# The float steps of an inverse square root on another engine: an encoder layer with 40 small calls of it

## The chip, the cores and the metric

The kernel runs on one core of a Trainium2 chip. A core has a matmul engine (TensorE, PE in the profile; its weight loads are PEld), a vector engine (VectorE, DVE), a scalar engine (ScalarE, ACT), a general engine (GpSimd, POOL) and a queue that issues most of the transfers (SyncE, SP). Each engine works through its own list of instructions in order; where one needs what another makes, it waits on a semaphore. The metric is the time of one execution on the device, in microseconds.

## The reference

One encoder layer is applied to two sequences, of 1024 and of 2048 tokens of width 1024, each with 16 learned meta tokens in front:

```python
xn = _rmsnorm(h, g_pre)
proj = xn @ w_in + b_in
ya = neighbourhood_attention(...) * silu(na_z) @ w_a      # 8 heads of 64
yb = mlstm(...) normalised per head * silu(ml_z) @ w_b    # 4 heads of 128, both directions
y = (ga * ya + gb * yb) @ w_out
return h + _rmsnorm(y, g_post)
```

An inverse square root is wanted at three places: for each token in the first norm of x, for each token and mLSTM head in the head norm (mean and variance over 128 channels), and for each token in the last norm. In each the argument is one number per token, so it has 128 partitions and 1 to 4 columns.

## The kernel before

All matmuls are made in pairs of a high and a low part (`mm3`, lines 141 to 146: three products for one), so most tiles are split by one ScalarE copy and one VectorE subtraction. Weights are loaded raw, split once (`wpump`, from line 221; the first three low parts are made by POOL, the others by VectorE, line 238) and kept in DRAM for later use.

Two generators are interleaved by estimated cost. The dense one (`dense`, `group`, `final`) makes the projections of x in halves of 512 tokens and, at the end of each sequence, the output projections in blocks of 512 tokens. The sparse one (`sparse`) makes the mLSTM of the prompt, its attention, then both of the sample. The instruction list of TensorE is exactly this order. Those of VectorE, ScalarE, POOL and SyncE are planned by the framework's scheduler from the data flow, with an estimate of each instruction's time, when the program is built; a changed instruction can therefore change the order of others on these engines.

The inverse square root is `rsqrt8` (line 125): an integer shift and an integer subtraction from a magic constant give a first guess (lines 130, 131), and three Newton passes of three VectorE instructions each improve it (lines 133 to 135). It is called 40 times from three places:

- `build_half`, line 295, 7 calls. 512 tokens of x are loaded in tiles `xr`, squared and summed by ScalarE (L292), the sums go through `rsqrt8`, VectorE scales x by the result (L298), TensorE transposes x (L309), ScalarE and VectorE split the transpose into `xh` (L311) and `xl` (L312). The first two calls stand at the start of the kernel, before any projection can be made.
- `ml_norm`, line 1193, 24 calls, one for each mLSTM head and 512 tokens. VectorE gates the head's output `hb` (L1184), takes its mean and variance (L1188, L1190), adds the epsilon (L1192); `rsqrt8` follows; VectorE normalises (four L1196) and gates again (L1197); eight steps of the generator later TensorE transposes the tile (L1202), ScalarE scales it (L1203), and it is stored.
- `final_out`, line 1369, 9 calls: five for 512 tokens at once, and in the last block of the sample one for each 128 tokens. ScalarE sums the squares of a block's output from PSUM (L1327), VectorE multiplies it by the gain (L1328), the sums are added (L1367, L1368), `rsqrt8` follows, VectorE scales and adds the input `xres` (L1373, twice for 128 tokens), and the result is stored (L1374). The four loads' buffers are reused, so a later `xres` is loaded when an earlier L1373 is done.

POOL does little else: it clears small tiles (L289, L361, L838, L840, L982 and others), copies 16 columns of meta keys (L362, L363), splits the three first weights, and issues the transfers of the attention's masks (L558, L636).

Of the kernel before, what the change touches and what calls it, by code (L numbers as in the profile page):

```python
# [13 lines left out]
ALU = mybir.AluOpType  # L14
# [96 lines left out]
class K:  # L111
# [13 lines left out]
    def rsqrt8(self, pool, v, shape):  # L125

        nc = self.nc
        y = pool.tile(shape, F32, name="nwy", bufs=2)
        t = pool.tile(shape, F32, name="nwt", bufs=2)
        nc.vector.tensor_scalar(y.bitcast(I32), v.bitcast(I32), 1, None, op0=ALU.logical_shift_right)  # L130
        nc.vector.tensor_scalar(y.bitcast(I32), y.bitcast(I32), -1.0, MAGIC, op0=ALU.mult, op1=ALU.add)
        for n in range(3):
            nc.vector.scalar_tensor_tensor(t, y, 0.25 ** n, y, op0=ALU.mult, op1=ALU.mult)
            nc.vector.tensor_tensor(t, t, v, op=ALU.mult)
            nc.vector.scalar_tensor_tensor(y, t, 3.0, y, op0=ALU.subtract, op1=ALU.mult)
        return y

    def psum(self, tag, shape):
# [1349 lines left out]
```

## Time and profile before

| | |
|---|---|
| median of 3 runs | 2904.53 us (2902.79 to 2905.13) |
| the profiled execution | 2912.43 us |
| its span on the core | 2910.7 us |
| TensorE busy | 2820.4 us, 97% |
| VectorE busy | 1749.4 us, 60% |
| ScalarE busy | 1293.7 us, 44% |
| POOL busy | 23.4 us, 1% |
| mean granted clock of TensorE | 0.989 |

The profile is one execution recorded by the hardware. Start times and durations are in us from the start of the span; `L133` is line 133 of the kernel; `nwt<-nwy` gives the tile written and the tiles read, then partitions x elements. `nwy` and `nwt` are the two tiles of `rsqrt8`. A note like `[12.93 <-DVE hb L1197]` behind a row says that the engine sat idle for 12.93 us before it and that VectorE's L1197 ended the wait. `x2` behind a row merges two like instructions. Durations of POOL are rough.

### The profile page before, as it was taken

The numbers are of one execution on the slowest core, as the hardware profiler recorded it, in microseconds if no ns is written. First come the engines' busy times: TensorE is split into PE (matmuls) and PEld (weight loads), VectorE is DVE, ScalarE is ACT, GpSimd is POOL, SyncE is SP. The second block draws the span as 40 slices with busy tenths as digits, with TensorE's granted clock in tenths as the row PEclk, the third lists the DMA queues.
The fourth block names the chain that finished last, engine by engine and source line by source line (L and its number), as shares of the span: only waits on it lengthen the run. The fifth ranks groups of instructions, "written<-read, shape, count | busy, mean of one in ns | idle before, by whom it ended". The sixth has DMA issues, their size and how long they took to land.

```text
span 2910.7 us, 49314 instructions
## 1 busy us (share of the span) xinstructions
PE 2820.4 (97%) x17488; PEld 2513.6 (86%) x17488; DVE 1749.4 (60%) x4813; ACT 1293.7 (44%) x3114; POOL 23.4 (1%) x107
## 2 busy tenths in 40 slices
PE   6999999999999999999998999999999999999998
PEld 6998898899789988888886988898888888889887
DVE  5232576666556755467669778463555557777843
ACT  4112555444343444355655545453444445545421
POOL 1000000000000000000000000000000000000000
PEclk9999999999999999999999999999999999999999
DMA  9655576754775553578779798546659659888975
GB/s 349 221 178 180 198 230 235 269 185 161 246 233 171 186 170 123 173 249 273 233 249 316 265 341 293 176 140 196 200 180 293 207 166 262 259 289 253 304 255 193
DMA packets 436888, 661.88 MB, mean 227 GB/s; under 512 B 51136, under 2 KB 257296, under 8 KB 436640
## 3 DMA queue, kind: packets, MB, share of 16 engines
q1 hardware_dynamic: 435520, 656.03, 68.9%
q0 software_dynamic: 1120, 2.69, 0.4%
q8 instruction: 138, 2.26, 0.3%
q14 instruction: 110, 0.90, 0.1%
HBM read 447.97 MB, written 210.61 MB: 226 GB/s over the span
## 4 chain that ended last, share of the span: by engine, by line
PE 83%; DMA 9%; DVE 5%; ACT 1%; issue 1%; SPq 0%; DVEq 0%; ACTq 0%
PE pj L144 14%; PE pj L145 14%; PE pj L146 14%; PE pj L409 6%; PE pj L410 6%; PE pj L411 6%; PE sm L700 3%; PE pj L1302 3%; PE pj L1300 3%; PE pj L1301 3%; PE tr L688 3%; PE sc L663 1%; PE sc L664 1%; DMA tg<-gt 1%; PE sm L146 1%
## 5 line engine op out<-in xcount | busy, mean ns | idle before, releaser
L144 PE MATMUL pj<-xh,whi 128*128 128x512 f32 (+1 forms) x1824 | 717.1, 393 | 0.2 <-DVE xl L312 0.2
L145 PE MATMUL pj<-xl,whi 128*128 128x512 f32 (+1 forms) x1824 | 700.3, 384 | 0.4 <-DVE xl L312 0.4
L146 PE MATMUL pj<-xh,wlo 128*128 128x512 f32 (+1 forms) x1824 | 698.5, 383 | 0.0
L409 PE MATMUL pj<-whi,xh 128*128 128x256 f32 (+3 forms) x1576 | 451.8, 287 | 0.0
L410 PE MATMUL pj<-wlo,xh 128*128 128x256 f32 (+3 forms) x1576 | 445.7, 283 | 0.0
L411 PE MATMUL pj<-whi,xl 128*128 128x256 f32 (+3 forms) x1576 | 445.4, 283 | 0.0
L146 PEld LDWEIGHTS pj<-xh,wlo 128*128 128x128 f32 x1824 | 343.9, 189 | 72.1
L144 PEld LDWEIGHTS pj<-xh,whi 128*128 128x128 f32 x1824 | 344.3, 189 | 57.7 <-DVE xl L312 0.8
L145 PEld LDWEIGHTS pj<-xl,whi 128*128 128x128 f32 x1824 | 344.7, 189 | 55.6 <-DVE xl L312 0.7
L409 PEld LDWEIGHTS pj<-whi,xh 128*128 128x128 f32 (+1 forms) x1576 | 295.5, 188 | 1.5 <-issue 0.2
L410 PEld LDWEIGHTS pj<-wlo,xh 128*128 128x128 f32 (+1 forms) x1576 | 295.2, 187 | 1.1
L411 PEld LDWEIGHTS pj<-whi,xl 128*128 128x128 f32 (+1 forms) x1576 | 295.1, 187 | 0.9
L1300 PE MATMUL pj<-whi,mh 128*128 128x256 f32 x768 | 221.7, 289 | 0.0
L671 ACT ACTIVATE prb<-sc,mx 128x384 f32<-128x384 f32 (+2 forms) x192 | 120.1, 625 | 228.1 <-DVE mx L667 221.3
L1302 PE MATMUL pj<-whi,mlo 128*128 128x256 f32 x768 | 218.8, 285 | 1.9 <-DVE mlo L1283 1.9
L1301 PE MATMUL pj<-wlo,mh 128*128 128x256 f32 x768 | 218.4, 284 | 0.0
L691 DVE TENSOR_TENSOR pts<-tr,pts 96x512 fp32r<-96x512 f32 (+2 forms) x192 | 131.9, 687 | 119.2 <-ACT pts L690 117.5
L418 DVE TENSOR_TENSOR stT<-pj,bb 128x256 f32<-128x256 f32 (+3 forms) x197 | 83.3, 423 | 153.7 <-PE pj L411 150.4
L690 ACT ACTIVATE pts<-tr 96x512 fp32r<-96x512 f32 (+2 forms) x192 | 114.0, 594 | 115.9 <-PE tr L688 115.6
L667 DVE CUSTOM_DVE_ANT_1 sc<-sc,gt 128x384 f32<-128x384 f32 (+2 forms) x192 | 118.7, 618 | 76.1 <-PE sc L664 68.3
L144 PE MATMUL pj<-yh,whi 128*128 128x512 f32 x384 | 157.0, 409 | 7.4 <-DVE tg L1279 7.3
L706 DVE TENSOR_TENSOR yg<-sm,yg 64x128 f32<-64x128 f32 x384 | 108.3, 282 | 77.7 <-ACT yg L704 70.1
(233 smaller groups left out, 5123.7 us busy)
## 6 DMA issues: line engine op xcount, KB each, us to landing
whi<-wh SPq DMA_DIRECT2D x176, 512.0 KB
wlo<-wl SPq DMA_DIRECT2D x176, 512.0 KB
wh<-whi SPq DMA_DIRECT2D x64, 512.0 KB
wl<-wlo SPq DMA_DIRECT2D x64, 512.0 KB
wraw<-w_in SPq DMA_DIRECT2D x48, 512.0 KB
gt<-st SPq DMA_DIRECT2D x96, 256.0 KB
tg<-gt SPq DMA_DIRECT2D x96, 256.0 KB
xh<-xh SPq DMA_DIRECT2D x6, 2048.0 KB
```

The costliest lines, as they stand in the source:

```text
L144: mm(out, ah, bh, start=start, stop=False)
L145: mm(out, ah, bl, start=False, stop=False)
L146: mm(out, al, bh, start=False, stop=stop)
L409: nc.tensor.matmul(o, xh, wh, start=k == 0, stop=False)
L410: nc.tensor.matmul(o, xh, wl, start=False, stop=False)
L411: nc.tensor.matmul(o, xl, wh, start=False, stop=k == KT - 1)
L667: nc.vector.tensor_tensor_reduce(out=so, in0=so, in1=gt[:, g0:g0 + ns, c0:c0 + 32], op0=ALU.add, op1=ALU.min, scale=-1.0, scalar=3.0e38, a ...
L671: nc.scalar.activation(pr_[:, :N].rearrange("p (b a c) -> p b a c", b=4, c=8), sc[:, :N].rearrange("p (a b c) -> p b a c", b=4, c=8), AF.E ...
L691: nc.vector.tensor_tensor(pts[:ks, :, 1, :], pt[:ks], pts[:ks, :, 0, :].bitcast(F32), op=ALU.subtract)
L1300: nc.tensor.matmul(o, mh[:, k, xs], wh, start=k == 0, stop=False)
L1301: nc.tensor.matmul(o, mh[:, k, xs], wl, start=False, stop=False)
L1302: nc.tensor.matmul(o, ml[:, k, xs], wh, start=False, stop=k == KT - 1)
```

## The change

Only the Newton passes change engine and form. The two integer steps stay on VectorE. Each pass was three VectorE instructions, of which two fold a constant in; it becomes four POOL instructions, since the constant and the subtraction of 3 are made by an instruction of their own. The values are the same up to rounding. A call so issues 2 instructions on VectorE and 12 on POOL, where it issued 11 on VectorE.

```diff
@@ -130,9 +130,10 @@
         nc.vector.tensor_scalar(y.bitcast(I32), v.bitcast(I32), 1, None, op0=ALU.logical_shift_right)
         nc.vector.tensor_scalar(y.bitcast(I32), y.bitcast(I32), -1.0, MAGIC, op0=ALU.mult, op1=ALU.add)
         for n in range(3):
-            nc.vector.scalar_tensor_tensor(t, y, 0.25 ** n, y, op0=ALU.mult, op1=ALU.mult)
-            nc.vector.tensor_tensor(t, t, v, op=ALU.mult)
-            nc.vector.scalar_tensor_tensor(y, t, 3.0, y, op0=ALU.subtract, op1=ALU.mult)
+            nc.gpsimd.tensor_tensor(t, y, y, op=ALU.mult)
+            nc.gpsimd.tensor_tensor(t, t, v, op=ALU.mult)
+            nc.gpsimd.tensor_scalar(t, t, 0.25 ** n, -3.0, op0=ALU.mult, op1=ALU.add)
+            nc.gpsimd.tensor_tensor(y, t, y, op=ALU.mult)
         return y
```

## The prediction

> **What bounds the kernel now.** I read the page first, then TensorE's waits, then every instruction that touches the two small tiles of the inverse square root, and last the timeline at the places where TensorE waits behind one.
>
> ```profile
> span 2910.7 us, 49314 instructions
> PE 2820.4 (97%) x17488; PEld 2513.6 (86%) x17488; DVE 1749.4 (60%) x4813; ACT 1293.7 (44%) x3114; POOL 23.4 (1%) x107
> ```
>
> TensorE is busy for 97% of the span, so a change off TensorE counts only where TensorE waits: the 90 us that are left. VectorE has 40% of its time free over the whole, POOL nearly all of it. The table of waits says which of those waits can lie behind an inverse square root (columns: total us, times, longest):
>
> ```profile
> PE pj L309 <- DVE xr L298: 22.7, 2, 18.1
> PE tr L1202 <- DVE hb L1197: 12.9, 1, 12.9
> ```
>
> The first is the start, where the first two calls are made and x is scaled by their result (L298). The second is one place in the middle where the head norm (L1196, L1197) comes late. The third place is the tail behind the last matmul, which no wait of TensorE shows. The tile view of the temporary counts the calls: three passes each, 120 instructions, so 40 calls.
>
> ```profile
> L133 DVE SCALAR_TENSOR_TENSOR nwt<-nwy x120: 140/161/166, 10.7 to 2905.1; 128x4 f32<-128x4 f32 x102, 128x1 f32<-128x1 f32 x12, 128x2 f32<-128x2 f32 x3, 128x3 f32<-128x3 f32 x3
> ```
>
> **The price of one call.** Removed: 9 instructions of VectorE per call, 360 in all. Their pace in a dependent chain stands in the tail, where nothing else runs beside them (timeline of VectorE, columns start and duration in us):
>
> ```profile
> 2893.48 0.15 DVE L131 TENSOR_SCALAR nwy<-nwy 128x1 int32<-128x1 int32 x1
> ...
> 2895.44 0.42 DVE L1328 TENSOR_TENSOR yo<-pj,gain 128x256 f32<-128x256 f32 x1 [0.64 <-ACT yo L1327]
> ...
> 2896.36 1.42 DVE L1373 SCALAR_TENSOR_TENSOR yo<-yo,nwy,xres 128x512 f32<-128x512 f32 x2
> ...
> 2903.96 0.15 DVE L133 SCALAR_TENSOR_TENSOR nwt<-nwy 128x1 f32<-128x1 f32 x1
> ...
> 2905.50 0.16 DVE L135 SCALAR_TENSOR_TENSOR nwy<-nwt,nwy 128x1 f32<-128x1 f32 x1
> 2905.70 0.75 DVE L1373 SCALAR_TENSOR_TENSOR yo<-yo,nwy,xres 128x512 f32<-128x512 f32 x1
> 2906.70 0.75 DVE L1373 SCALAR_TENSOR_TENSOR yo<-yo,nwy,xres 128x512 f32<-128x512 f32 x1 [0.25 <-DMA xres<-x_sample]
> ```
>
> The first of nine starts at 2903.96 and the reader of the result at 2905.70: 1.74 us per call, 0.193 us per step ((2905.50 - 2903.96) / 8). Added: 12 dependent instructions of POOL per call, 480 in all, and two hand-overs between engines. The trace holds no arithmetic of POOL this small; its nearest rows are these copies of 16 elements.
>
> ```profile
> 332.05 0.20 POOL L362 COPY km<-st 128x16 f32<-128x16 f32 x1 [2.22 <-ACT st L345]
> 332.18 0.20 POOL L363 COPY km<-st 128x16 f32<-128x16 f32 x1
> ...
> 340.18 0.15 POOL L361 MEMSET km<- 128x64 f32 x1 [0.40 <-DMA nkm<-km]
> 340.39 0.46 POOL L362 COPY km<-st 128x16 f32<-128x16 f32 x1
> ```
>
> A copy lasts 0.20, and a copy onto the tile just cleared starts 0.06 after the clearing ends (340.33 to 340.39). I take 0.26 us per step. The lower end is 0.13, the spacing of the two copies at 332 that do not depend on each other. For the upper end one piece of work is made by both engines, the low half of a weight tile:
>
> ```profile
> L238 DVE TENSOR_TENSOR wlo<-wraw,whi 128x1024 fp32r<-128x1024 f32 x61 | 74.5, 1221 | 58.2 <-ACT whi L235 58.1
> L238 POOL TENSOR_TENSOR wlo<-wraw,whi 128x1024 fp32r<-128x1024 f32 x3 | 7.1, 2353 | 12.2 <-ACT whi L235 12.2
> ```
>
> POOL needs 1.93 times as long; 1.93 x 0.193 = 0.37 us per step. I stay at 0.26, since these tiles have 1 to 4 elements and the copy's row is the nearest in size. One call then costs 0.13 (VectorE to POOL: the row at 14.25 below ends at 14.41, POOL follows at 14.54) + 12 x 0.26 = 3.12 + 0.13 back, taken equal: **3.4 us instead of 1.7**, where nothing else is in the way.
>
> **The lock between the two engines.** The copy at 340.39 took 0.46 instead of 0.20, and it ran while VectorE worked on this:
>
> ```profile
> 340.37 0.43 DVE L1050 TENSOR_TENSOR kl<-kf,kh 128x256 fp32r<-128x256 f32 x1 [0.20 <-ACT kh L1049]
> ```
>
> Both end within 0.05 us (340.80, 340.85). The start shows it the other way round: a tiny VectorE instruction of two SBUF inputs lasts 2.30 while POOL splits a weight.
>
> ```profile
> 10.54 0.17 DVE L131 TENSOR_SCALAR nwy<-nwy 128x2 int32<-128x2 int32 x1
> ...
> 11.47 2.34 POOL L238 TENSOR_TENSOR wlo<-wraw,whi 128x1024 fp32r<-128x1024 f32 x1 [10.34 <-ACT whi L235]
> 11.52 2.30 DVE L134 TENSOR_TENSOR nwt<-nwt,ss 128x2 f32<-128x2 f32 x1
> ...
> 14.25 0.16 DVE L134 TENSOR_TENSOR nwt<-nwt,ss 128x2 f32<-128x2 f32 x1
> ...
> 14.54 0.10 POOL L289 MEMSET ss<- 128x5 f32 x1 [0.73 <-DVE nwt L134]
> 14.65 4.62 DVE L298 SCALAR_TENSOR_TENSOR xr<-xr,nwy,gain 128x1024 f32<-128x1024 f32 x2
> 14.65 2.34 POOL L238 TENSOR_TENSOR wlo<-wraw,whi 128x1024 fp32r<-128x1024 f32 x1
> ...
> 18.13 1.12 PE L309 MATMUL pj<-ident,xr 128*128 128x128 f32 x4 [18.13 <-DVE xr L298]
> ...
> 21.42 0.17 DVE L131 TENSOR_SCALAR nwy<-nwy 128x3 int32<-128x3 int32 x1
> ...
> 24.80 3.66 DVE L298 SCALAR_TENSOR_TENSOR xr<-xr,nwy,gain 128x1024 f32<-128x1024 f32 x3
> ```
>
> So one of the two stands until the other has finished. The Trainium skill has this as a rule (SBUF — State Buffer, Who interferes with whom): a VectorE instruction with two SBUF inputs and a GpSimd one that reads SBUF exclude each other for a whole instruction; the trace agrees (2.30 and 0.46 us). By that rule the tail term below is +4.5; by engines that never block each other it would be +0.5, and the sum 4 us lower.
>
> **Start.** Before, L131 ends at 10.71 and L298 starts at 14.65, the 2.30 us stall included. After, the chain and two weight splits share POOL's queue. Taking one split inside the chain: 10.71 + 3.4 + 2.34 = 16.4. The second split then holds the lock to about 18.7, and L298 adds 1.2 (3.66 / 3): 19.9 against 18.13, **+1.7**. With no split inside, L298 stands only for the first and ends at 17.7 (-0.4); with steps of 0.37, +3.0. The second call has POOL to itself: 21.59 + 3.4 = 25.0 against 24.80, **+0.2** (-1.4 to +1.5). All that TensorE does later is shifted by this. Start: +1.9, between -1.8 and +4.5.
>
> **Tail.** Four calls, one per 128 rows, now stand in one queue, and L1373 (two SBUF inputs, 1.42 a pair) stops POOL in between. First result: 2893.63 + 3.4 = 2897.0. Each further one 3.12 + 1.42 = 4.5 later: 2901.5, 2906.0, 2910.5, as each next L131 is ready before POOL is free. The last pair of L1373 ends 1.5 later at 2912.0, before at 2907.45: **+4.5**; the store behind it is unchanged. At 0.13 per step POOL keeps up and the load of xres still sets the end at 2906.70 (0); at 0.37 it is +10.
>
> **Middle.** Here the change can win. The head norm's chain is cut up between large VectorE instructions that stand in the same queue:
>
> ```profile
> 1526.84 0.68 DVE L1197 TENSOR_TENSOR hb<-hb,szg 128x512 f32<-128x512 f32 x1
> ...
> 1557.91 0.17 DVE L131 TENSOR_SCALAR nwy<-nwy 128x4 int32<-128x4 int32 x1
> ...
> 1559.65 0.16 DVE L133 SCALAR_TENSOR_TENSOR nwt<-nwy 128x4 f32<-128x4 f32 x1
> ...
> 1568.81 0.16 DVE L135 SCALAR_TENSOR_TENSOR nwy<-nwt,nwy 128x4 f32<-128x4 f32 x1
> ...
> 1569.15 1.10 DVE L1196 TENSOR_SCALAR hb<-hb,mv,nwy 128x128 f32<-128x128 f32 x4
> ...
> 1571.17 0.68 DVE L1197 TENSOR_TENSOR hb<-hb,szg 128x512 f32<-128x512 f32 x1
> ```
>
> ```profile
> 1572.00 1.09 PE L1202 MATMUL tr<-ident,hb 128*128 128x128 f32 x4 [12.93 <-DVE hb L1197]
> ```
>
> ```profile
> 1515.00:1600.00 85.00, 71.49 (x379) 60.93 (x377) 78.03 (x228) 49.38 (x116) 0.10 (x1) 0.92 0.93 315
> ```
>
> The stretch's row has VectorE busy 78.03 of 85 us, and nine steps take 11 us. On POOL: 1558.08 + 3.4 = 1561.5, and about 0.2 for each of twelve steps for the lock (the copy above lost 0.26): 1563.9. L1196 can then start 5.3 earlier: **-5.3**. Ends: -12.9, the whole wait; +2.4, if the planner leaves L1196 where it is and twelve POOL steps of 0.2 us each stop VectorE.
>
> **The rest.** Of the 23 other head norms, the one with the least room ends at 1527.52, and TensorE takes its result 2.7 us later:
>
> ```profile
> 1530.24 0.62 PE L1202 MATMUL tr<-ident,hb 128*128 128x128 f32 x4
> ```
>
> 3.4 - 1.7 + 2.4 = 4.1 would pass that by 1.4 only if its chain were not also cut up; I cost it at nothing. The same for the other five scalings of x and the five earlier output norms. VectorE loses 360 x 0.16 = 58 us of work and can be stopped for up to 480 x 0.2 = 96 us; with 1161 us idle both are put at 0, at -2 to +3. No DMA is moved, but POOL's clears and mask loads now stand behind calls of 3.4 us, hidden by buffers filled a block ahead. That the work stays on VectorE after all cannot be: the engine is named in each instruction.
>
> **Sum:** 1.9 + 4.5 - 5.3 = +1.1 us. The profiled execution took 2912.43 (span 2910.7), 8 us over the median of the runs, 2904.53; on that median: **2905.6 us**.
>
> **Rivals.** *The late head norm disappears* (faster): VectorE, freed of the small steps in that stretch, catches up and TensorE finds hb ready. For it: everything late there is late by queueing. Against: other steps of the same chain are late too, L131 at 1557.91. Time: 1.9 + 4.5 - 12.9 = -6.5, 2898.0. *POOL's step is slow* (slower): at 0.37 us start and tail cost 4.5 + 10, the middle still gives 4: +10.5, 2915.0. For it: the 1.93; against: the copy's 0.20. It decides from 0.32 us per step, where the sum passes 5.8 us. The Trainium skill (GPSIMD Engine Reference, Performance versus the Vector engine) puts a two-input GpSimd operation at 1.96 times VectorE's; the trace agrees for the large tile (1.93). *The middle gives nothing* (slower): the instruction orders of VectorE, ACT and the queues are planned anew, and L1196 may come no earlier: +6.4, 2910.9.
>
> **How the numbers follow.** A measurement of this kernel can tell about 0.2%, 5.8 us, from no change. Forecast 0.44; late norm gone 0.18; slow step 0.23; nothing in the middle 0.15, a quarter of it inside 5.8 us. Of the forecast's 0.44 some 0.02 falls beyond the bound on each side. So faster 0.18 + 0.02 = 0.20, slower 0.23 + 0.11 + 0.02 = 0.36, same 0.40 + 0.04 = 0.44. The forecast's own range is 2899 to 2910; the range over all goes from below the first rival to beyond the slow step (1.9 and 4.5 at their upper ends with no gain: +14.5): 2896 to 2919.
>
> **What would show it.** Right: VectorE's busy time near 1690, POOL's above 100 us; POOL starts of nwt 0.26 apart; L298's first end near 19.9; last L1373 near 2912; the wait of L1202 near 7.6. Wrong: steps beyond 0.32, a new wait behind L1196 or L1373, or TensorE's waits on tg and prb grown by new orders.

## The result and the profile after

The changed kernel takes 2910.82 us (median of 20 runs, 2907.36 to 2916.9), the kernel before 2905.51 us (20 runs, 2901.14 to 2910.74). The ratio is 1.002 with an interval of 1.0013 to 1.0026: 5.3 us slower, between 3.8 and 7.5. The forecast was +1.1 us and 2905.6 us. The time lies inside the range, and 5.3 us is just below the bound of 5.8 us that was set for "no change"; but the interval leaves out the forecast's +1.1, so some terms of the sum were wrong. The largest is "the rest", which had been put at 0.

A reader of the two profiles alone would be misled. The profiled execution of the kernel after took 2907.36 us, the lowest of its runs, and that of the kernel before 2912.43, above all 20 of its own. TensorE makes the same matmuls in both, yet it was busy for 2810.7 us in the one, at a mean granted clock of 0.992, and for 2820.4 in the other, at 0.989. The time in which it stood idle goes the way of the medians: 94.9 us after and 90.3 before. Terms are therefore measured stretch by stretch, and totals are taken from medians and from TensorE's idle time.

In the kernel after, lines behind 135 have numbers higher by one (L298 is L299, L1202 is L1203, L1373 is L1374). The head of its page:

```profile
span 2905.6 us, 49418 instructions
PE 2810.7 (97%) x17488; PEld 2504.4 (86%) x17488; DVE 1695.4 (58%) x4453; ACT 1296.0 (45%) x3114; POOL 136.0 (5%) x587
```

VectorE lost 360 instructions and 54 us, POOL won 480 and 113 us. Its tile view of the temporary, as of before:

```profile
L133 POOL TENSOR_TENSOR nwt<-nwy x120: 189/200/1117, 10.7 to 2899.9; 128x4 f32<-128x4 f32 x102, 128x1 f32<-128x1 f32 x12, 128x2 f32<-128x2 f32 x3, 128x3 f32<-128x3 f32 x3
```

A step takes 0.19 to 0.20 us whether it has one column or four; the longest of this line, 1.12 us, stood behind a VectorE instruction. TensorE's waits:

```profile
PE pj L310 <- DVE xr L299: 21.5, 2, 20.4
PE tr L1203 <- DVE hb L1198: 9.4, 1, 9.4
```

The first transposes of x wait for 20.4 us instead of 18.1, the late head norm costs 9.4 instead of 12.9.

**The start.** POOL in the kernel after, rows of the first call and of the second:

```profile
10.72 0.19 POOL L133 TENSOR_TENSOR nwt<-nwy 128x2 f32<-128x2 f32 x1 [9.58 <-DVE nwy L131]
10.99 0.20 POOL L134 TENSOR_TENSOR nwt<-nwt,ss 128x2 f32<-128x2 f32 x1
...
11.71 2.35 POOL L239 TENSOR_TENSOR wlo<-wraw,whi 128x1024 fp32r<-128x1024 f32 x1
14.02 0.19 POOL L133 TENSOR_TENSOR nwt<-nwy 128x2 f32<-128x2 f32 x1
14.17 2.34 POOL L239 TENSOR_TENSOR wlo<-wraw,whi 128x1024 fp32r<-128x1024 f32 x1
16.47 0.19 POOL L134 TENSOR_TENSOR nwt<-nwt,ss 128x2 f32<-128x2 f32 x1
...
18.05 0.19 POOL L133 TENSOR_TENSOR nwt<-nwy 128x3 f32<-128x3 f32 x1 [0.23 <-DVE nwy L131]
...
18.79 0.20 POOL L136 TENSOR_TENSOR nwy<-nwt,nwy 128x2 f32<-128x2 f32 x1
18.95 0.20 POOL L135 TENSOR_SCALAR nwt<-nwt 128x3 f32<-128x3 f32 x1
19.23 1.13 POOL L136 TENSOR_TENSOR nwy<-nwt,nwy 128x3 f32<-128x3 f32 x1
20.44 1.12 POOL L133 TENSOR_TENSOR nwt<-nwy 128x3 f32<-128x3 f32 x1
...
23.34 0.20 POOL L136 TENSOR_TENSOR nwy<-nwt,nwy 128x3 f32<-128x3 f32 x1
```

Both weight splits stand inside the first call's chain, not one, and the second call's first steps stand between the last steps of the first. The chain runs from 10.72 to 18.99. VectorE's scalings that wait for the two calls:

```profile
15.34 1.22 DVE L173 TENSOR_SCALAR bfh<-bfm 128x52 f32<-128x52 f32 x1 [4.70 <-DMA bfm<-b_fm]
...
19.02 2.48 DVE L299 SCALAR_TENSOR_TENSOR xr<-xr,nwy,gain 128x1024 f32<-128x1024 f32 x2 [1.05 <-POOL nwy L136]
23.57 3.67 DVE L299 SCALAR_TENSOR_TENSOR xr<-xr,nwy,gain 128x1024 f32<-128x1024 f32 x3 [2.06 <-POOL nwy L136]
```

The first scaling starts 4.4 us later than before (14.65), but lasts 1.3 instead of 3.4, since no split is left to hold it: the first transposes come 2.2 us later (20.36 against 18.13). The second starts 1.2 us earlier (24.80), because POOL can begin the second call at 18.05, where L131 ended at 21.59 before: ScalarE now squares the last small tile of x (L293) at 16.11, and before it did so at 19.78, behind its first copy of a transpose. That is an order planned anew, not POOL's doing. By the matmul that stood at 50.0 us the kernel after is 1.75 us behind.

**The middle.** The same head norm as before, VectorE:

```profile
1560.42 0.18 DVE L131 TENSOR_SCALAR nwy<-nwy 128x4 int32<-128x4 int32 x1
...
1566.30 1.11 DVE L1197 TENSOR_SCALAR hb<-hb,mv,nwy 128x128 f32<-128x128 f32 x4
...
1570.28 0.69 DVE L1198 TENSOR_TENSOR hb<-hb,szg 128x512 f32<-128x512 f32 x1
```

From the end of L131 to the normalisation it takes 5.7 us (1560.60 to 1566.30) instead of 11.1 (1558.08 to 1569.15). But the gating behind it, L1198, now comes 4.0 us after the normalisation's start and not 2.0: six other groups of VectorE instructions were planned in between, where there were two.

**The tail.** POOL, the first steps and the last step of the first tile's call, and steps of the second beside it:

```profile
2886.08 0.20 POOL L133 TENSOR_TENSOR nwt<-nwy 128x1 f32<-128x1 f32 x1 [81.20 <-DVE nwy L131]
2886.35 0.19 POOL L134 TENSOR_TENSOR nwt<-nwt,sv 128x1 f32<-128x1 f32 x1
...
2889.10 0.19 POOL L133 TENSOR_TENSOR nwt<-nwy 128x1 f32<-128x1 f32 x1
2889.24 0.19 POOL L136 TENSOR_TENSOR nwy<-nwt,nwy 128x1 f32<-128x1 f32 x1
2889.38 0.19 POOL L134 TENSOR_TENSOR nwt<-nwt,sv 128x1 f32<-128x1 f32 x1
2889.66 0.61 POOL L135 TENSOR_SCALAR nwt<-nwt 128x1 f32<-128x1 f32 x1
2890.35 0.58 POOL L136 TENSOR_TENSOR nwy<-nwt,nwy 128x1 f32<-128x1 f32 x1
2891.01 0.19 POOL L133 TENSOR_TENSOR nwt<-nwy 128x1 f32<-128x1 f32 x1
```

and VectorE's four pairs of output scalings there:

```profile
2889.47 1.42 DVE L1374 SCALAR_TENSOR_TENSOR yo<-yo,nwy,xres 128x512 f32<-128x512 f32 x2 [0.61 <-POOL nwy L136]
...
2893.16 1.41 DVE L1374 SCALAR_TENSOR_TENSOR yo<-yo,nwy,xres 128x512 f32<-128x512 f32 x2 [1.31 <-POOL nwy L136]
...
2897.26 1.41 DVE L1374 SCALAR_TENSOR_TENSOR yo<-yo,nwy,xres 128x512 f32<-128x512 f32 x2 [1.73 <-POOL nwy L136]
...
2900.95 1.41 DVE L1374 SCALAR_TENSOR_TENSOR yo<-yo,nwy,xres 128x512 f32<-128x512 f32 x2 [2.27 <-POOL nwy L136]
```

Every pair waits for POOL last, none for a load: POOL's queue is the bound of the tail, as forecast, but the pairs follow at 3.69, 4.10 and 3.69 us and not at 4.5. From the end of the last matmul to the end of the span it takes 12.63 us (2892.96 to 2905.6), before 10.06 (2900.60 to 2910.66): +2.6.

### The profile page after: what moved, and what is told of

Its sections match the earlier page's. It is cut to its first block, busy times and chain, and to the rows that moved or that the text cites. A ratio compares the mean times of both kernels' runs of the same rounds, so it can differ in the third digit from the quotient of the medians.

```text
span 2905.6 us, 49418 instructions
## 1 busy us (share of the span) xinstructions
PE 2810.7 (97%) x17488; PEld 2504.4 (86%) x17488; DVE 1695.4 (58%) x4453; ACT 1296.0 (45%) x3114; POOL 136.0 (5%) x587
## 4 chain that ended last, share of the span: by engine, by line
PE 82%; DMA 7%; DVE 5%; issue 3%; POOL 1%; ACT 1%; SPq 1%; DVEq 0%; POOLq 0%; ACTq 0%
PE pj L145 14%; PE pj L146 14%; PE pj L147 14%; PE pj L410 6%; PE pj L412 6%; PE pj L411 6%; PE sm L701 3%; PE tr L689 3%; PE pj L1301 3%; PE pj L1303 3%; PE pj L1302 3%; PE sc L664 1%; PE sc L665 1%; PE sm L147 1%; DMA whi<-wh 1%
```

## The experiments

TensorE's list of matmuls is the same in all these kernels, so the time between two matmuls, found by their places in the list, can be compared from kernel to kernel. In this table the stretches are named by where they begin and end in the kernel before; "start" runs from 0 to the matmul that stood at 50.0 us, "end" from the last matmul's end to the span's end. All in us, worked out from the starts of those matmuls in one profiled execution each. The last column is the span less TensorE's busy time: how long TensorE stood idle in the whole execution.

| kernel | start | 300 to 800 | of it 750 to 800 | 800 to 850 | 1500 to 1580 | end | TensorE idle |
|---|---|---|---|---|---|---|---|
| before | 50.0 | 500.0 | 49.95 | 50.10 | 80.0 | 10.06 | 90.3 |
| e8, before again | 50.2 | 501.2 | 50.73 | 51.59 | 79.6 | 9.92 | 89.0 |
| after | 51.8 | 503.1 | 52.97 | 49.75 | 76.7 | 12.63 | 94.9 |
| e4, after again | 52.6 | 504.6 | 52.74 | 48.50 | 76.4 | 12.64 | 95.9 |
| e1 | 49.5 | 506.3 | 54.17 | 49.00 | 76.9 | 9.74 | 94.1 |
| e2 | 53.4 | 499.5 | 49.66 | 49.13 | 79.9 | 12.66 | 93.9 |
| e3 | 50.1 | 503.9 | 52.24 | 49.09 | 76.9 | 9.79 | 92.6 |
| e5 | 50.0 | 500.0 | 49.86 | 49.73 | 74.2 | 9.96 | 86.4 |
| e6 | 50.1 | 502.0 | 50.84 | 49.06 | 79.2 | 9.92 | 91.4 |
| e7 | 49.6 | 505.9 | 52.80 | 50.06 | 74.9 | 12.64 | 91.5 |
| e9 | 52.3 | 502.2 | 51.69 | 50.12 | 76.1 | 9.74 | 86.8 |
| e10 | 49.9 | 502.3 | 53.03 | 48.25 | 79.3 | 9.74 | 88.7 |
| e11 | 52.6 | 504.9 | 52.91 | 49.30 | 78.6 | 10.24 | 90.3 |
| e12 | 53.3 | 499.8 | 50.27 | 53.23 | 80.7 | 9.73 | 94.6 |

Two profiles of one kernel show what one execution is worth: from 2500 to 2600 it was 100.1 us in before and 97.9 in e8, and from 800 to 850 it was 50.1 and 51.6. So a difference of 2 us in one stretch of one profile is weak; one that comes back in several kernels is not. The idle times scatter by some us too: e11 has no more than before, though its median is 3.7 us higher.

Most variants give `rsqrt8` a flag that chooses the old form on VectorE:

```diff
-    def rsqrt8(self, pool, v, shape):
+    def rsqrt8(self, pool, v, shape, vec=False):
...
+        if vec:
+            for n in range(3):
+                nc.vector.scalar_tensor_tensor(t, y, 0.25 ** n, y, op0=ALU.mult, op1=ALU.mult)
+                nc.vector.tensor_tensor(t, t, v, op=ALU.mult)
+                nc.vector.scalar_tensor_tensor(y, t, 3.0, y, op0=ALU.subtract, op1=ALU.mult)
+            return y
```

The three callers pass it: `build_half`, `ml_norm`, `final_out`. Line numbers behind it are higher by seven than before's.

**First set: the ends, the norms, and the change once more.** The theory was that start and tail (the first two and the last four calls) lose and that the 24 head norms win; the rival, that what the norms win is given back where orders change.

*e1: first two and last four calls back on VectorE.*

```diff
-            r = self.rsqrt8(wp, ss[:, :m], [P, m])
+            r = self.rsqrt8(wp, ss[:, :m], [P, m], vec=True if xp else False)
-        r = self.rsqrt8(fp, sv[:, a:b], [P, b - a])
+        r = self.rsqrt8(fp, sv[:, a:b], [P, b - a], vec=True if b - a == 1 else False)
```

> The first two calls and the last four are back on VectorE; the other 34 stay on POOL. If the cost of the change lies at the start and in the tail (in the two profiles the first transposes are 1.2 us later by the 24th matmul, and the stretch behind the last matmul is 12.6 instead of 10.1 us) and the late head norm in the middle gains 3 to 5 us, this kernel is 2 to 5 us faster than the kernel before, and 4 us or more faster than the change as a whole. If the cost lies in the middle (new orders on VectorE, ScalarE and the queues), it is slower than the kernel before by 2 us or more, with the ends as before.

Measured: 2908.47 us against 2904.91, 1.0011 (1.0001 to 1.0020). The ends are back at the old times in the table (49.5 and 9.74), and it is 5.1 us faster than e4 beside it. But it isn't faster than before: with start and tail repaired and the wait of the middle still at 9.6 us, it loses 3.6 us by the medians (0.3 to 5.8 by the interval), and TensorE idles 4.5 us more than in before (94.1 and the mean of 90.3 and 89.0). So something outside the three places costs the change several microseconds.

*e2: only those six calls on POOL*, the two conditions the other way round and `vec=True` in `ml_norm`.

> Only the first two calls and the last four are on POOL; the other 34 are on VectorE as before. If the ends are the cost: 3 to 6 us slower than the kernel before, the tail 2.5 us longer and the first matmuls about 1 us later, the wait before L1202 near 13 us as before. If the cost is in the middle: within 3 us of the kernel before, although the tail shows its 2.5 us.

Measured: 2912.05 us, 1.0018 (1.0005 to 1.0031), so 1.5 to 9 us slower. Start +3.4 and end +2.6 in the table, 6.0 together; the stretch from 300 to 800 is untouched. The ends theory holds in its place, and its size lies within the interval.

*e3: only the 24 head norms on POOL*, `vec=True` in the other two callers.

> Only the 24 calls of the head norm are on POOL. If moving them shortens the wait before L1202 (12.9 before, 9.4 after the change) and costs nothing elsewhere: 3 to 5 us faster than the kernel before. If the rival holds (the middle gives nothing or costs): no faster, with the wait above 11 us or with new waits of the same size on other tiles.

Measured: 2905.1 us, 0.9998 (0.9988 to 1.0009). No faster, as the rival had it. The table shows the gain from 1500 on (-3.1 against before) and a place where some is given back: 300 to 800, +3.9 against before and +2.7 against e8. The 2.3 of it between 750 and 800 shrink to 1.3 by 850.

*e4: the change, unaltered, a second time.*

> The change once more, for its profile: the two profiles shown so far stand 5 us the other way round than the medians. If the difference in the middle is made by the new orders, its waits (9.4 before L1202, 5.2 behind prb, 21.5 behind the scaling of x) come again within 1 us; those that come out otherwise by several us belong to the execution and not to the change. Time: 3 to 7 us above the kernel before.

Measured: 2913.58 us, 1.0028 (1.0018 to 1.0039). The waits for xr and hb come back (21.2 and 9.6 us in total), and so does the longer stretch from 300 to 800; a wait for the attention's `prb`, 5.2 us in the first profile, was 8.9 here and is a matter of the execution.

**Second set: which norms, and the start without POOL's splits.**

*e5: only the sample's 16 head norms on POOL*, in `ml_norm`:

```diff
-        rs = self.rsqrt8(mp, mv[:, :, 1], [P, 4])
+        rs = self.rsqrt8(mp, mv[:, :, 1], [P, 4], vec=s == 0)
```

> Only the 16 head-norm calls of the sample are on POOL. With all 24 on POOL the time was that of the kernel before: the stretch around the late head norm (1500 to 1580 us) was 3 us shorter, the stretch from 750 to 800 us, at the end of the prompt's mLSTM, 2 to 4 us longer. If these two belong to the calls near them: 3 us faster than the kernel before, wait before L1202 near 10, the stretch at 750 near 50 us. If they do not (an order planned anew shifts things anywhere): the stretch at 750 stays at 52 or more although no call before it has moved, and the time stays within 2 us.

*e6: only the prompt's eight*, `vec=s == 1`.

> Only the 8 head-norm calls of the prompt are on POOL: the other half. If the costs belong to the calls near them: 2 to 4 us slower than the kernel before, the stretch from 750 to 800 us at 52 to 54 instead of 50, the wait before L1202 at 13 as before. If the stretch at 750 us is not theirs: within 2 us, with 50 us there.

Measured: e5 2904.27 us against 2906.41, 0.9994 (0.9981 to 1.0007); e6 2906.51, 1.0004 (0.9992 to 1.0015). In e5 the middle gains 5.9 us (wait 9.0) and 300 to 800 is as before: a norm moved near a place acts at that place, and the stretch at 750 does not feel norms that come later. In e6 the middle has its old wait of 12.9, and 300 to 800 is 2.0 above before but only 0.8 above e8. So the prompt's norms may cost some of what e3 lost there, but this pair doesn't show it. The e5 time cannot be told from before.

*e7: the change, with the first three weight splits on VectorE*, so that POOL has the start to itself.

```diff
-                eng = nc.vector if self.nu > 4 else nc.gpsimd
+                eng = nc.vector
```

> The change, with the first three weight splits on VectorE instead of POOL, so that nothing else stands in POOL's queue at the start. If the start's delay is the splits inside the chain (two of 2.35 us each, 10.72 to 19.0): the first call is done near 14.2 us, the first transposes start near 15.6 instead of 20.4 (before: 18.1), and the time falls by 1 to 5 us against the change. If instead POOL's own steps make the delay: the first transposes no earlier than 18 us.

Measured: 2913.31 us, 1.0025 (1.0012 to 1.0037). No gain shows. POOL in e7 at the start:

```profile
11.28 0.19 POOL L135 TENSOR_SCALAR nwt<-nwt 128x2 f32<-128x2 f32 x1
11.56 1.07 POOL L136 TENSOR_TENSOR nwy<-nwt,nwy 128x2 f32<-128x2 f32 x1
...
13.26 1.10 POOL L135 TENSOR_SCALAR nwt<-nwt 128x2 f32<-128x2 f32 x1
```

Two steps stand behind VectorE's splits, which take 1.22 us each there, so the first transposes come at 17.16 and not at the 15.6 expected. By the matmul at 50 us e7 is still 2.2 us ahead of the change, but its ratio lies beside those of the change, 1.0020 and 1.0028: what was gained at the start can't be seen in the time. Its interval is wide enough to hide 2 us.

*e8: the kernel before, a second time.*

> The kernel before once more, for a second profile of it: its first one has 9 us more between 2500 and 2600 us than the changed kernel's, which the medians do not show. If that belongs to the execution, this profile has 96 us or less in a stretch of 100 us there that the first passed in 100; the stretch at 750 us stays near 50, the wait before L1202 near 13, the tail near 10. Time: within 0.1% of the kernel before.

Measured: 2906.67 us, 0.9998 (0.9984 to 1.0011). It shows how far two executions of one kernel differ (table). The stretch from 2500 to 2600 took 97.9 us and not 96 or less, and so only a part of that difference is shown to be the execution's.

**Third set: what is left, and the tail's lock alone.**

*e9: e5 and e7's splits together.*

> The sample's 16 head-norm calls on POOL, everything else on VectorE, the first three weight splits too: the parts that gained in the profiles, without those that cost. If the gains of the stretches add up (3 to 6 us around the late head norm, 1 to 3 us at the start, nothing lost in the tail): 4 to 8 us faster than the kernel before. If what is gained in one stretch is given back in others: within 3 us of it.

*e12: the kernel before with e7's splits.*

> The kernel before, with only the first three weight splits on VectorE instead of POOL. If the 2.3 us that one of its tiny steps stood behind a split is paid by TensorE: the first transposes 1 to 2.5 us earlier than 18.1, and 1 to 3 us faster as a whole. If what follows at the start (loads of x) decides: the transposes earlier, the time within 1 us.

Measured: e9 2906.73 us, 1.0010 (0.9997 to 1.0022); e12 2909.19, 1.0015 (1.0005 to 1.0025). In both the first transposes come 2 us earlier (16.20, 16.15), and both are behind by the matmul at 50 us (52.3, 53.3). The gains of e9 didn't add up to a faster kernel, though TensorE idles less in it than in before (86.8). e12 fits neither of its cases: by its interval it is 1.5 to 7 us slower. VectorE in e12:

```profile
22.25 0.69 DVE L312 TENSOR_TENSOR xl<-pj,xh 128x512 fp32r<-128x512 f32 x1 [3.46 <-ACT xh L311]
...
25.64 3.67 DVE L298 SCALAR_TENSOR_TENSOR xr<-xr,nwy,gain 128x1024 f32<-128x1024 f32 x3
29.24 1.21 DVE L238 TENSOR_TENSOR wlo<-wraw,whi 128x1024 fp32r<-128x1024 f32 x1
30.37 0.67 DVE L312 TENSOR_TENSOR xl<-pj,xh 128x512 fp32r<-128x512 f32 x1
...
32.77 1.20 DVE L238 TENSOR_TENSOR wlo<-wraw,whi 128x1024 fp32r<-128x1024 f32 x1
```

The second scaling starts 0.8 us later than before (25.64 against 24.80), and two splits stand on VectorE among the `xl` that the first projections need: the third of the three, and the fourth, which came at 40.08 before. So earlier first transposes alone don't make the start shorter; the second group and what stands around it on VectorE come last.

*e10: the five later scalings of x and the five whole-block output norms on POOL, all else on VectorE*, e1's conditions with `vec=True` in `ml_norm`.

> Only the five later scalings of x and the five output norms of whole blocks are on POOL. With them on VectorE too the stretch from 300 to 800 us was 499.5 to 501.2 us long, with the prompt's head norms on POOL 502.0 and 503.9, with all on POOL 503.1 to 506.3. If these ten calls have a cost of their own: 1 to 4 us slower than the kernel before, that stretch above 501.5. If not: within 1.5 us, the stretch as before.

Measured: 2907.66 us, 1.0010 (1.0 to 1.002): some 3 us by the ratio, 1.3 by the medians, at the edge of what can be told from none. 300 to 800 is 2.3 above before and 1.1 above e8; the part from 750 is 53.03, 2.3 to 3.1 above. But the 50 us behind it are 1.9 to 3.3 shorter (48.25), so that 750 to 850 takes 101.3 and lies between before (100.1) and e8 (102.3). TensorE idles no more in it than in before (88.7). A cost of these ten calls is not shown.

*e11: the change, with the lock of the tail taken away.* For the last 512 tokens ScalarE scales, and the addition of x is left out, so no two-input VectorE instruction of that size stands there.

```diff
-            nc.vector.scalar_tensor_tensor(y, y, r[:, tt - a:tt - a + 1], xr[j], op0=ALU.mult, op1=ALU.add)
+            if b - a == 1:
+                nc.scalar.activation(y, y, AF.Copy, scale=r[:, tt - a:tt - a + 1])
+            else:
+                nc.vector.scalar_tensor_tensor(y, y, r[:, tt - a:tt - a + 1], xr[j], op0=ALU.mult, op1=ALU.add)
```

> The change, but in the last block of the sample (512 tokens) ScalarE scales the result and the input x is not added: that part of the output is left out, so that VectorE has no instruction of two SBUF inputs in the tail. If the lock is what stretches POOL's chain there (steps of 0.58 to 0.61 instead of 0.19): no such step, four chains 3.3 us apart instead of 3.7 to 4.1, the stretch behind the last matmul 10.5 to 11.3 instead of 12.6 us. If those steps are slow for another reason: they come again, and the stretch stays above 12.

Measured: 2910.06 us, 1.0011 (0.9998 to 1.0025). The end falls from 12.63 to 10.24, below the 10.5 to 11.3 expected. ScalarE in e11:

```profile
2897.46 1.34 ACT L1375 ACTIVATE yo<-yo,nwy 128x512 f32<-128x512 f32 x2 [1.68 <-POOL nwy L136]
...
2900.34 1.33 ACT L1375 ACTIVATE yo<-yo,nwy 128x512 f32<-128x512 f32 x2 [1.18 <-POOL nwy L136]
...
2903.76 1.33 ACT L1375 ACTIVATE yo<-yo,nwy 128x512 f32<-128x512 f32 x2 [1.73 <-POOL nwy L136]
2906.64 1.33 ACT L1375 ACTIVATE yo<-yo,nwy 128x512 f32<-128x512 f32 x2 [1.54 <-POOL nwy L136]
```

Pairs follow 2.9 to 3.4 us apart, each still behind POOL, and no POOL step from 2894 on is longer than 0.19 us. The lock in the tail is shown: with the two-input scalings gone, the stretched steps are gone.

## Why the prediction was near, and which terms were off

**Start, forecast +1.9.** Measured +1.75 in the first profile, +2.6 in e4, and +3.4 in e2, where these calls move with only the tail's. By TensorE's idle time in this stretch it is +1.7 (means of 25.2 and 24.0 after, 23.1 and 22.8 before). The size holds, the working only partly. "Taking one split inside the chain" was wrong: both splits stood in it, so the first transposes are 2.2 us late and not 1.7. And "the second call +0.2" came as -1.2, since ScalarE's new order lets it begin 3.5 us earlier, which the working had not asked about.

**Tail, forecast +4.5.** Measured +2.6, in four kernels alike (12.63 to 12.66 against 9.7 to 10.1). The mechanism is right: POOL's queue ends every pair, and the VectorE scalings stop POOL (e11). The step 0.26 us is nearly right: POOL's starts are 0.27 us apart (2886.08 and 2886.35; ten such intervals take 2.74). The failed term is "L1373 stops POOL in between" at its full 1.42: each of the two instructions of a pair delays one POOL step, 0.61 and 0.58 instead of 0.19, so 0.8 us per pair. Twelve steps and this make 3.3 + 0.8 = 4.1, and 4.10 is measured where no step of the next call stands ahead of this call's last one; 3.69 is measured where one does, as at 2889.10, so that it costs the next call nothing. The Trainium skill (SBUF — State Buffer, Who interferes with whom) has the exclusion last for a whole instruction; the trace agrees (0.61 and 0.58 us), but between the two instructions of a pair POOL got its turn, and the forecast had taken the pair for one.

**Middle, forecast -5.3.** Measured -3.2 (the stretch from 1500, means of two each) to -3.5 (the wait, 12.9 to 9.4). The part worked out was right: -5.4 from L131 to the normalisation, and locked steps did cost (0.49 and 0.52 us beside the usual 0.20), though the chain took 4.0 us (1560.68 to 1564.69) and not 5.8, and VectorE's queue took the rest. What failed is the unsaid assumption that the gating (L1197) keeps its distance behind the normalisation (L1196). It came 4.0 us after the start of the normalisation instead of 2.0. So the third rival, orders planned anew, was right in a part: it took two of the five microseconds back.

**The rest, forecast 0, -2 to +3.** This is the step that failed most: VectorE's saved work and POOL's stops, with 1161 us of VectorE idle, "both are put at 0". e1, which has only this and the middle, is 3.6 us slower than before. TensorE's idle time gives the size for the change as a whole: it rises by 5.8 us (95.4, the mean of after and e4, against 89.6, the mean of before and e8), and start, middle and tail make up 0.9 of that. So 4.9 us are idle time elsewhere. The medians leave 3.8 for the rest (5.3 less 1.5, the stretch times of start, middle and tail in the table), 2.3 to 6.0 by the interval. Both lie above the upper bound of +3, though the interval reaches below it.

Where they lie is not settled. In time, 300 to 800 is 3.3 us longer (means of two each, 503.9 and 500.6), and most of that falls between 750 and 800. The rows of this stretch, from the same matmul to the same matmul, for before, e8, after and e4 (columns: busy time of PE, PEld, DVE, ACT and POOL, granted clock, DMA share, GB/s):

```profile
750.05:800.00 49.95, 47.30 (x224) 37.72 (x223) 22.70 (x53) 20.00 (x35) 0.00 (x0) 0.97 0.89 312
750.64:801.37 50.73, 47.26 (x224) 37.76 (x223) 22.66 (x53) 20.11 (x35) 0.00 (x0) 0.97 0.88 307
751.87:804.84 52.97, 45.72 (x224) 36.52 (x223) 19.96 (x35) 20.15 (x35) 7.28 (x32) 1.00 0.92 308
754.52:807.26 52.74, 48.16 (x224) 38.39 (x223) 20.64 (x37) 20.34 (x35) 7.28 (x32) 0.94 0.93 312
```

The two executions of the changed kernel are longer here for different reasons. TensorE idles 2.7 and 3.5 us in the first two rows, 7.3 in after and 4.6 in e4; in e4 the same 224 matmuls took 48.16 us at a granted clock of 0.94, and in after 45.72 at 1.00. TensorE's waits in this stretch in before:

```profile
PE sc L663 <- ACT kd L643: 2.0, 1, 2.0
PE sc L664 <- DVE kx L645: 0.5, 1, 0.5
```

and in after:

```profile
PE sc L664 <- ACT kd L644: 2.7, 1, 2.7
PE pj L310 <- DVE xl L313: 2.0, 2, 1.6
PE pj L147 <- DMA wlo<-wl: 2.0, 1, 2.0
PE sc L665 <- DVE kx L646: 0.5, 1, 0.5
```

The new wait for a weight that lands late, 2.0 us, is 0.5 in e4. It doesn't come back in that size, so it isn't the cause of what comes back. The DMA engines are busy for 88 to 93% of the stretch in all four, so a transfer issued later has little slack to land in; that this matters is argued, not shown. VectorE, which the prediction looked at for room, is idle for some 60% of it in after and e4.

Calls of either kind planned near this place lengthen the stretch (e3 with norms alone, e10 without them), calls far from it don't (e5, e2); e6 (50.84) and e9 (51.69) lie between. But the next 50 us give most of it back: from 750 to 850, after and e4 take 102.0 us (mean), before and e8 101.2, and e12, which has no call on POOL, 103.5. So a cost at this place isn't shown. By idle time the 4.9 us fall on 300 to 800 (+4.0) and on 2600 to the last matmul (+3.2), less 1.3 from 800 to 1500 and 1.0 from 1580 to 2600. One kernel's two executions differ by up to 3 us in such a stretch. What does it stays open: orders planned anew are a guess, since no run held the orders of the queues fixed.

**The sum.** By TensorE's idle time, means of after and e4 against before and e8: start +1.7, middle -3.4, tail +2.6, the rest +4.9, together +5.8. The medians say +5.3 (and +8.7 in the repeat, e4, whose interval begins at 5.2). The forecast had +1.9 - 5.3 + 4.5 + 0 = +1.1: the tail was 1.9 too dear, the middle 1.9 too good, the rest 4.9 too cheap. The three places worked out make +0.9 and not +1.1, but that is two errors of the same size which cancel, and so it is luck.

**The rivals.** The late norm did not disappear (9.4 us left). POOL's step was not slow: 0.27, under the 0.32 from which that rival decides. The Trainium skill's 1.96 (GPSIMD Engine Reference, Performance versus the Vector engine) holds for the large tile, 1.93 as the prediction showed; for these tiles a step takes 0.27 / 0.193 = 1.4 times as long. Orders planned anew came true in a part, in the middle; the rest, +4.9, had not been looked for, and that it is new orders too is argued, not shown.

## What to carry to other kernels

Moving small dependent steps to an idle engine paid here only where the chain was being cut up by other work on the old engine: the six calls at the two ends stood bare and lost 5 us, one call won 3, and the other 33 lay in cover, yet TensorE idled some 5 us more outside these places. So ask not only which calls are bare: the calls in cover, put at 0, were the largest error of the sum. Where one profiled execution differs from the next by as much as the effect, compare the same two matmuls in every kernel, trust only what returns, look whether the next stretch gives it back, and set TensorE's idle time beside the total, since its busy time differed here by 9.7 us for the same matmuls.

## What was not expected of the hardware

- A VectorE instruction with one SBUF input, L173, 128x52, lasted 1.22 us while POOL's split ran, and ended 0.05 us after it (16.56 against 16.51). In the kernel before the same instruction lasted 0.17, with no split beside it. The prediction had counted on the lock for two inputs alone. The Trainium skill (SBUF — State Buffer, Who interferes with whom) says that `tensor_scalar` can enter a mode that takes both ports and then excludes GpSimd; the row agrees.
- Large VectorE instructions of two inputs hold a POOL step for 1.07 to 1.13 us (L299, and the splits in e7), smaller ones for 0.5 to 0.6 (L1374, and those of the middle). POOL doesn't always get its turn between two of them. In the kernel after, a step that started at 1583.64 ended only at 1584.66, behind both of two such instructions that ended at 1584.60 (e4 has the same step of 1.02 us):

```profile
1583.64 1.02 POOL L135 TENSOR_SCALAR nwt<-nwt 128x4 f32<-128x4 f32 x1
1583.84 0.76 DVE L1098 TENSOR_TENSOR sl<-um,sh 128x256 fp32r<-128x256 f32 x2
```

- Hand-overs are cheaper than the 0.13 us assumed: VectorE to POOL 0.09 (2885.99, the end of L131, to 2886.08), POOL to VectorE 0.04 (2889.43 to 2889.47).
